# A two-layer decoder trunk on one core: matmul operands moved to multiples of 256 bytes, residual updates raised in VectorE's queue, 24 weight remainders formed by DMA, and matmuls of ones put first

## The chip, the core and the metric

The kernel runs on one core of a Trainium2 chip. The metric is the device time of one execution in microseconds (us); a run before and a run after are compared by their medians. The engines are TensorE (PE: matmuls; PEld: its weight loads), VectorE (DVE), ScalarE (ACT), GpSimd (POOL) and SyncE (SP, which issues most DMAs). Each engine works off its own queue in order.

## The reference

The program computes two layers (DEPTH = 2) over 512 tokens of width 1024 in float32. Each layer has three steps, each added to the residual `x`:

```python
x = x + 0.5 * swiglu(rmsnorm(x, ffn1_norm[l]), w_gate, w_up, w_down)   # FFN of width 2816
x = x + hybrid_mixer(rmsnorm(x, mix_norm[l]), ...)                     # sparse attention | mLSTM heads, then w_out
x = x + 0.5 * swiglu(rmsnorm(x, ffn2_norm[l]), w_gate, w_up, w_down)
# swiglu(x) = (silu(x @ w_gate) * (x @ w_up)) @ w_down
```

So there are four FFNs and two mixers. The mixer has a projection of 3020 columns, an indexer that keeps 128 keys for each query, softmax attention, an mLSTM and an output projection.

## The kernel before

**Number format.** Every large product runs as three matmuls in a faster float32 form (`mm3`): each operand is split into a rounded part `hi` and a remainder `lo`, and `hi*hi + hi*lo + lo*hi` is accumulated. Three matmuls of one such product are called a triple below. A weight tile (a unit, 128 x 1024) comes by an SP DMA into `raw` (six buffers); `unit()` lets ACT round it into `whi` (line 267) and makes the remainder `wlo = raw - whi`. Mostly DVE does that (line 272). For units that are marked (the third field of a job) ACT writes `-whi` into `wlo` (line 269) and a DMA issued by POOL adds the weights from memory on top (line 270). Before, only units of the mixers were marked. `whi` and `wlo` have three buffers each, and units are prepared two ahead of the one in use.

**FFN.** `ffn_plan` lays out the order: gate and up units of block 0 (`U 0`, four units), then two units of block 1, two down units of block 0 (`D 0`), two more units of block 1, then groups of two blocks in which each block is seven products (`quad`, a Strassen-like scheme on halves of 256 columns, line 495) with down units (line 547, through `mm3`) between them. One `U` unit is 8 triples of 512 columns. One down unit of block 0 has four products of two triples, and each product goes to one of three PSUM buffers `aux`, which DVE empties by adding it to the residual (line 550, called an x update here). In the same stretch DVE works off `combine()`: scaled inputs `ys` (line 383), sums of halves `yc` (line 391) and remainders `yl`, `s4a` and `qT` (line 401), all needed by the later quads. The code of `combine()` stands ahead of the x updates, and a scheduler orders each engine's queue by priority, which follows the order of the code except where `high_priority` raises it.

**Where operands lie.** Tiles of the pool `act` get their place in SBUF in the order in which their tags are first used. In the built program the tiles `kT`, `big` and `h` (tag `s4b`), and `whi` and `wlo`, begin at multiples of 256 bytes in each partition; `qT` begins 64 bytes past one; `yh0` to `yh7`, `yl0` to `yl7`, `zah`, `zal` and the four `s4a` begin 128 bytes past one.

**Start.** SP issues x, three weight units, x in the other layout and a dozen small constants before the fourth weight unit. The tile `ones` is set by POOL.

Of the kernel before, what the change touches and what calls it, by code (L numbers as in the profile page):

```python
# [7 lines left out]
F32 = mybir.dt.float32  # L8
F32R = mybir.dt.float32r
I32 = mybir.dt.int32  # L10
AF = mybir.ActivationFunctionType
ALU = mybir.AluOpType
# [3 lines left out]
P = 128  # L16
S = 512
# [3 lines left out]
NKT = D // P  # L21
# [3 lines left out]
AH, AD = 8, 64  # L25
# [7 lines left out]
UN = 1024  # L33
# [2 lines left out]
HEADS = (("o", 0), ("qk", 0), ("qk", 1), ("qk", 2), ("o", 1), ("qk", 3), ("o", 2), ("o", 3))  # L36
PLAIN = ((0, 0), (0, 1), (1, 0), (1, 1))
H = S // 2
RAWS = 6
PRODUCTS = (("a11", "b11", 0, True), ("s2", "t2", 1, True), ("a12", "b21", 0, False), ("s1", "t1", 2, True),  # L40
            ("s3", "t3", 1, False), ("a22", "t4", 3, True), ("s4", "b22", 2, False))
# [17 lines left out]
class Trunk:  # L59
# [49 lines left out]
    def setup(self):  # L109
        nc, cp, t = self.nc, self.cp, self.t  # L110
        self.x = []
        self.stream = []
        self.jobs = []
        self.last = []
        self.plan = self.ffn_plan()
        for l in range(DEPTH):
            self.ffn_units(l, "1")
            n0 = len(self.jobs)
            for u in range(4):
                self.add(t["w_a"][l, u], 2 * C_A)  # L120
            for nm in ("w_q", "w_v"):
                for u in range(4):
                    self.add(t[nm][l, u])
            for nm, h in HEADS:
                if nm == "o":
                    self.add(t["w_o"][l, h])
                else:
                    for i in range(2):
                        self.add(t["w_qk"][l, 2 * h + i])
            for u in range(8):  # L130
                self.add(t["w_out"][l, u])
            for i in POOLU:
                self.jobs[n0 + i] = self.jobs[n0 + i][:2] + (True,)
            self.ffn_units(l, "2")
        self.made = 0
        self.loaded = []
        self.taken = 0
        self.raws = []
        self.g1 = []
        for l in range(DEPTH):  # L140
            g = cp.tile([P, NKT], F32, name=f"g1_{l}", tag=f"g1_{l}")
            nc.scalar.dma_start(g, t["g1"][l])
            self.g1.append(g)
        warm = cp.tile([P, 1], F32, name="warm", tag="warm")
        nc.vector.memset(warm, 0.0)
        nc.scalar.activation(warm, warm, AF.Silu)
        with self.tc.high_priority(offset=20000):
            for i in range(NKT):
                xt = cp.tile([P, S], F32, name=f"x{i}", tag=f"x{i}")
                nc.sync.dma_start(xt, t["x"][i])  # L150
                self.x.append(xt)
                if i in START:
                    self.fetch()
            self.xt = []
            for b in range(NB):
                xt = self.ap_.tile([P, D], F32, name="xt", tag=("s4b", "s4b", "so", "so")[b], bufs=2)
                nc.sync.dma_start(xt, t["xt"][b])
                self.xt.append(xt)

        def const(nm, shape, src):  # L160
            c = cp.tile(shape, F32, name=nm, tag=nm)
            nc.sync.dma_start(c, src)
            return c

        self.zid = cp.tile([P, 3 * P], F32R, name="zid", tag="zid")
        z = self.tmp()[:, 0:3 * P]
        nc.sync.dma_start(z, t["ident"])
        nc.scalar.activation(self.zid, z, AF.Copy)
        z = self.zid.bitcast(F32)
        self.ident = z[:, P:2 * P]  # L170
        self.pick = cp.tile([32 + MH, MH], F32R, name="pick", tag="pick")
        nc.vector.tensor_tensor(out=self.pick, in0=z[0:32 + MH, P:P + MH], in1=z[0:32 + MH, P + 32:P + 32 + MH],
                                op=ALU.add)
        self.ones = cp.tile([P, P], F32, name="ones", tag="ones")
        nc.gpsimd.memset(self.ones, 1.0)
        self.abias = const("abias", [P, P], t["abias"])
        self.rope = const("rope", [P, NB, 2 * AD], t["rope"])
        self.gm = [const(f"gm_{l}", [P, NKT], t["gm"][l]) for l in range(DEPTH)]
        self.g2 = [const(f"g2_{l}", [P, NKT], t["g2"][l]) for l in range(DEPTH)]
        self.cw = [const(f"cw_{l}", [P, 8, 5], t["cw"][l]) for l in range(DEPTH)]  # L180
        self.mn = [const(f"mn_{l}", [P, MH], t["mn"][l]) for l in range(DEPTH)]
# [12 lines left out]
                plan += [("D", gi - 1, u) for n, u in at if n == 7]  # L194
        return plan + [("D", len(GROUPS) - 1, u) for u in range(4)]

    def add(self, src, n=UN):
        self.jobs.append((self.plain, (self.raw(src, n), n), False))

    def raw(self, src, n=UN):  # L200
        self.stream.append((src, n))
# [3 lines left out]
    def ffn_units(self, l, n):  # L205
        t = self.t
        for kind, b, i in self.plan:
            if kind == "U":
                m, u = PLAIN[i]
                self.add(t["w" + "gu"[m] + n][l, b, u])  # L210
            elif kind == "D":
                self.add(t["wda" + n][l, i] if b == 0 else t["wdb" + n][l, b - 1, i])
            else:
                if i == 0:
                    q = {}
# [322 lines left out]
    def ffn_down(self, h, nf, u):  # L538
        nc = self.nc
        w = UN // nf  # L540
        hi, lo = self.unit()
        for j in range(w // P):
            d = u * (w // P) + j
            ps = self.pa.tile([P, S], F32, name="aux", tag="aux")
            for f in range(nf):
                c = slice(f * w + j * P, f * w + (j + 1) * P)
                self.mm3(ps, (hi[:, c], lo[:, c]), (h[0][:, f, :], h[1][:, f, :]), f == 0, f == nf - 1)
                if f % 2:
                    self.tick()
            nc.vector.scalar_tensor_tensor(self.x[d], ps, 0.5, self.x[d], op0=ALU.mult, op1=ALU.add)  # L550


    def mixer(self, l):
# [594 lines left out]
```

## Time and profile before

| | |
|---|---|
| time, median of 3 runs (lowest to highest) | 1961.65 us (1958.77 to 1962.58) |
| time of the profiled execution | 1961.55 us |
| its span, first to last instruction | 1959.9 us |
| mean granted TensorE clock | 0.988 |
| PE busy | 1911.9 us, 98% of the span |
| VectorE busy | 1394.3 us, 71% |
| ScalarE busy | 943.7 us, 48% |
| GpSimd busy | 511.2 us, 26% |

Busy time of TensorE counts from a matmul's start to its modelled end, and consecutive matmuls overlap; so a busy share near 100% says that matmuls followed each other without a gap, not how quickly. How quickly is read from the distances between their starts. Waits of TensorE, with what ended them, are in the view of waits.

### The profile page before, as it was taken

The numbers are of one execution on the slowest core, as the hardware profiler recorded it, in microseconds if no ns is written. First come the engines' busy times: TensorE is split into PE (matmuls) and PEld (weight loads), VectorE is DVE, ScalarE is ACT, GpSimd is POOL, SyncE is SP. The second block draws the span as 40 slices with busy tenths as digits, with TensorE's granted clock in tenths as the row PEclk, the third lists the DMA queues.
The fourth block names the chain that finished last, engine by engine and source line by source line (L and its number), as shares of the span: only waits on it lengthen the run. The fifth ranks groups of instructions, "written<-read, shape, count | busy, mean of one in ns | idle before, by whom it ended". The sixth has DMA issues, their size and how long they took to land.

```text
span 1959.9 us, 29399 instructions
## 1 busy us (share of the span) xinstructions
PE 1911.9 (98%) x11672; PEld 1698.4 (87%) x11672; DVE 1394.3 (71%) x2242; ACT 943.7 (48%) x1481; POOL 511.2 (26%) x306
## 2 busy tenths in 40 slices
PE   8899999999999999999999999999999999999999
PEld 6799999887887799999878999998888877999997
DVE  7866667589955886666788666665898558866665
ACT  5344344577765444343444343446677644443432
POOL 0332322212113132333203423312211121433330
PEclk9899999999999999999999999999999999999999
DMA  7132323474346232322321323334643452332322
GB/s 256 58 109 95 120 76 126 117 152 108 87 108 140 76 108 76 119 100 94 119 86 61 123 81 114 109 112 125 146 108 87 109 128 65 108 108 87 121 74 86
DMA packets 60473, 209.82 MB, mean 107 GB/s; under 512 B 7984, under 2 KB 8496, under 8 KB 60336
## 3 DMA queue, kind: packets, MB, share of 16 engines
q1 hardware_dynamic: 51696, 178.44, 27.1%
q0 software_dynamic: 8064, 29.36, 9.2%
q8 instruction: 91, 1.49, 0.3%
q14 instruction: 46, 0.38, 0.1%
q10 hardware_dynamic: 576, 0.15, 0.1%
HBM read 205.83 MB, written 2.10 MB: 106 GB/s over the span
## 4 chain that ended last, share of the span: by engine, by line
PE 85%; DVE 10%; ACT 2%; issue 2%; POOL 0%; DMA 0%; DVEq 0%; SPq 0%; ACTq 0%; POOLq 0%
PE mm L495 36%; PE aux L289 26%; PE mm L289 22%; DVE sc L843 2%; PE op L289 1%; DVE m L842 1%; DVE wlo L272 1%; PE aux L892 1%; DVE yl L401 0%; DVE x L1075 0%; DVE yc L391 0%; DVE sc L832 0%; DVE x L550 0%; DVE big L332 0%; ACT tmp L329 0%
## 5 line engine op out<-in xcount | busy, mean ns | idle before, releaser
L267 ACT ACTIVATE whi<-raw 128x1024 fp32r<-128x1024 f32 (+1 forms) x292 | 308.3, 1056 | 478.7 <-PE aux L289 213.3
L272 DVE TENSOR_TENSOR wlo<-raw,whi 128x1024 fp32r<-128x1024 f32 (+1 forms) x236 | 309.8, 1313 | 102.0 <-ACT whi L267 98.2
L244 POOL TENSOR_TENSOR ws<-raw 128x1024 f32<-128x1024 f32 x72 | 194.5, 2702 | 641.5 <-DVE wlo L272 457.1
L495 PE MATMUL mm<-yh,wlo 128*128 128x256 f32 x1152 | 324.5, 282 | 0.0
L495 PE MATMUL mm<-yl,whi 128*128 128x256 f32 x1152 | 324.5, 282 | 0.0
L495 PE MATMUL mm<-yh,whi 128*128 128x256 f32 x1152 | 324.3, 282 | 0.0
L272 DVE TENSOR_TENSOR wlo<-ws,whi 128x1024 fp32r<-128x1024 f32 x144 | 219.0, 1521 | 98.3 <-ACT whi L267 98.1
L267 ACT ACTIVATE whi<-ws 128x1024 fp32r<-128x1024 f32 x144 | 152.8, 1061 | 264.2 <-PE mm L495 127.1
L550 DVE SCALAR_TENSOR_TENSOR x<-aux,x 128x512 f32<-128x512 f32 x192 | 129.9, 686 | 136.2 <-PE aux L289 135.9
L495 PEld LDWEIGHTS mm<-yh,whi 128*128 128x128 f32 x1152 | 216.9, 188 | 2.0 <-ACT pT L516 0.7
L495 PEld LDWEIGHTS mm<-yl,whi 128*128 128x128 f32 x1152 | 216.7, 188 | 1.4
L495 PEld LDWEIGHTS mm<-yh,wlo 128*128 128x128 f32 x1152 | 216.9, 188 | 0.0
L495 PE MATMUL mm<-qT,whi 128*128 128x256 f32 x1152 | 205.6, 280 | 0.7 <-DVE lg L527 0.7
L495 PEld LDWEIGHTS mm<-qT,whi 128*128 128x128 f32 x1152 | 177.8, 188 | 3.8 <-issue 1.4
L495 PE MATMUL mm<-qT,wlo 128*128 128x256 f32 x576 | 160.8, 279 | 0.0
L289 PE MATMUL aux<-zah,whi 128*128 128x512 f32 x384 | 151.6, 395 | 0.0
L289 PE MATMUL aux<-zal,whi 128*128 128x512 f32 x384 | 151.6, 395 | 0.0
L289 PE MATMUL aux<-zah,wlo 128*128 128x512 f32 x384 | 151.6, 395 | 0.0
L244 POOL TENSOR_TENSOR ws<-ws,raw 128x1024 f32<-128x1024 f32 x36 | 89.8, 2493 | 115.9 <-issue 115.6
L495 PEld LDWEIGHTS mm<-qT,wlo 128*128 128x128 f32 x576 | 108.1, 188 | 0.0
L289 PE MATMUL mm<-yh,whi 128*128 128x512 f32 x256 | 106.4, 416 | 0.0
L495 PE MATMUL mm<-s4a,whi 128*128 128x256 f32 x576 | 104.7, 282 | 0.0
(287 smaller groups left out, 4216.5 us busy)
## 6 DMA issues: line engine op xcount, KB each, us to landing
raw<-wg_dram SPq DMA_DIRECT2D x88, 512.0 KB, 3.6
raw<-wu_dram SPq DMA_DIRECT2D x88, 512.0 KB, 3.7
raw<-wdb_dram SPq DMA_DIRECT2D x80, 512.0 KB, 3.6
raw<-w_qk_dram SPq DMA_DIRECT2D x16, 512.0 KB, 3.2
wlo<-w_qk_dram POOLq DMA_DIRECT2D x16, 512.0 KB, 5.4
raw<-w_out_dram SPq DMA_DIRECT2D x16, 512.0 KB, 3.2
wlo<-w_out_dram POOLq DMA_DIRECT2D x16, 512.0 KB, 5.8
raw<-wda_dram SPq DMA_DIRECT2D x8, 512.0 KB, 3.6
```

Of the source, the lines that this page charges most:

```text
L244: self.tc.keep_in_program_order(self.nc.gpsimd.tensor_tensor(out=out, in0=x, in1=y, op=op))
L267: nc.scalar.activation(hi[:, :n], raw, AF.Copy)
L272: nc.vector.tensor_tensor(out=lo[:, :n], in0=raw, in1=hi[:, :n].bitcast(F32), op=ALU.subtract)
L289: self.nc.tensor.matmul(ps, lhsT, rhs, start=start, stop=stop)
L495: nc.tensor.matmul(ps[:, f, :], a[:, c], r, start=first and f == 0 and k == 0 and n == 0, stop=k == 3 and n == 2, skip_group_check=True)
L550: nc.vector.scalar_tensor_tensor(self.x[d], ps, 0.5, self.x[d], op0=ALU.mult, op1=ALU.add)
L842: nc.vector.max(out=m8, in_=sc)
L843: nc.vector.match_replace(out=sc, in_to_replace=m8, in_values=sc, imm_value=MARK)
L892: nc.tensor.transpose(pt[:, j * P:(j + 1) * P], it["lg"][:, j * P:(j + 1) * P], self.ident)
```

## The change

Four edits.

1. In `setup`, the tags of the operand tiles of the pool `act` (`yh`, `yl`, `zah`, `zal`, `kT`, `qT`, `s4a`, `s4b`) are used first, in an order in which all of them begin at multiples of 256 bytes (read from the built program; `big` too). Nothing is computed by it.
2. The x update of a down unit is issued with a raised priority.
3. Six units of each FFN, the four of block 1 and the two of `D 0`, get their remainder from ACT and an accumulating POOL DMA in place of DVE.
4. `ones` is set ahead of the loads, and 16 matmuls of `ones` by `ones` (128 x 128) stand first in TensorE's queue. Their result is not used.

```diff
+WARM = 16
@@ setup
+        for tag, shape, n in ([(f"y{c}{i}", [P, S], 1) for i in range(NKT) for c in "hl"] +
+                              [("zah", [P, 4, S], 1), ("zal", [P, 4, S], 1), ("kT", [P, 4, S], 1),
+                               ("qT", [P, AH, S], 1), ("s4a", [P, S], 4), ("s4b", [P, UN], 2)]):
+            for _ in range(n):
+                self.ap_.tile(shape, F32R, name=tag, tag=tag, bufs=n)
         warm = cp.tile([P, 1], F32, name="warm", tag="warm")
         nc.vector.memset(warm, 0.0)
         nc.scalar.activation(warm, warm, AF.Silu)
+        self.ones = cp.tile([P, P], F32, name="ones", tag="ones")
+        nc.gpsimd.memset(self.ones, 1.0)
+        with self.tc.manual_schedule(engines={mybir.EngineType.PE}):
+            ps = self.pa.tile([P, S], F32, name="aux", tag="aux")
+            for _ in range(WARM):
+                self.mm(ps[:, 0:P], self.ones, self.ones, True, True)
...
-        self.ones = cp.tile([P, P], F32, name="ones", tag="ones")
-        nc.gpsimd.memset(self.ones, 1.0)
@@ add, ffn_units
-    def add(self, src, n=UN):
-        self.jobs.append((self.plain, (self.raw(src, n), n), False))
+    def add(self, src, n=UN, dma=False):
+        self.jobs.append((self.plain, (self.raw(src, n), n), dma))
...
-                self.add(t["w" + "gu"[m] + n][l, b, u])
+                self.add(t["w" + "gu"[m] + n][l, b, u], dma=b == 1)
             elif kind == "D":
-                self.add(t["wda" + n][l, i] if b == 0 else t["wdb" + n][l, b - 1, i])
+                self.add(t["wda" + n][l, i] if b == 0 else t["wdb" + n][l, b - 1, i], dma=b == 0)
@@ ffn_down
-            nc.vector.scalar_tensor_tensor(self.x[d], ps, 0.5, self.x[d], op0=ALU.mult, op1=ALU.add)
+            with self.tc.high_priority(offset=500):
+                nc.vector.scalar_tensor_tensor(self.x[d], ps, 0.5, self.x[d], op0=ALU.mult, op1=ALU.add)
```

Each engine's order changes only in the first part of each FFN (and at the program's start). VectorE in the first FFN, around the first x updates, before (`x_83` is the first of the eight tiles of x, `yl` and `s4a` are remainders of combine):

```order
L391 TENSOR_TENSOR yc<-ys,yc 128x512 x2
L401 TENSOR_TENSOR yl_353<-ys,yh_352 128x512
L401 TENSOR_TENSOR yl_345<-yc,yh_344 128x512
L401 TENSOR_TENSOR yl_347<-yc,yh_346 128x512
L401 TENSOR_TENSOR yl_355<-ys,yh_354 128x512
L391 TENSOR_TENSOR ys<-ys 128x2x256 x2
L391 TENSOR_TENSOR yc<-yc,ys 128x512 x2
L401 TENSOR_TENSOR yl_365<-yc,yh_364 128x512
L401 TENSOR_TENSOR yl_367<-yc,yh_366 128x512
L550 SCALAR_TENSOR_TENSOR x_83<-aux,x_83 128x512
L550 SCALAR_TENSOR_TENSOR x_87<-aux,x_87 128x512
```

The same place now (`x_131` is the first tile of x; L561 is the x update, L411 and L401 are combine, L485 a step of the gate of block 1):

```order
L401 TENSOR_TENSOR yc<-ys,yc 128x512 x2
L481 TENSOR_TENSOR lg<-mm,rsb 128x512 x2
L411 TENSOR_TENSOR yl_393<-yc,yh_392 128x512
L561 SCALAR_TENSOR_TENSOR x_131<-aux,x_131 128x512
L485 TENSOR_TENSOR lg<-lg,rsb 128x512
L411 TENSOR_TENSOR yl_395<-yc,yh_394 128x512
L561 SCALAR_TENSOR_TENSOR x_135<-aux,x_135 128x512
L485 TENSOR_TENSOR lg<-lg,rsb 128x512
L561 SCALAR_TENSOR_TENSOR x_137<-aux,x_137 128x512
L411 TENSOR_TENSOR yl_401<-ys,yh_400 128x512
L561 SCALAR_TENSOR_TENSOR x_139<-aux,x_139 128x512
L411 TENSOR_TENSOR yl_403<-ys,yh_402 128x512
```

The first x update stood behind all sums and eight remainders of combine; it now stands behind four sums and three remainders, and the rest alternates with the following x updates. In the other three FFNs it stands behind all of combine (one pair, `s4a`, more than before), but without the five weight remainders (line 272) that lay between.

ScalarE in the first FFN, where the first marked units are prepared, before (`rsb` is the row of inverse norms that the gate waits for):

```order
L168 ACTIVATE zid<-tmp 128x384
L267 ACTIVATE whi<-raw 128x1024 x3
L365 ACTIVATE rsb<-aux 128x512
L474 ACTIVATE lg<-lg 128x512 x2
L267 ACTIVATE whi<-raw 128x1024
```

And now:

```order
L180 ACTIVATE zid<-tmp 128x384
L277 ACTIVATE whi<-raw 128x1024 x2
L279 ACTIVATE wlo<-whi 128x1024
L277 ACTIVATE whi<-raw 128x1024
L279 ACTIVATE wlo<-whi 128x1024
L375 ACTIVATE rsb<-aux 128x512
```

Two more activations (L279, the negated `whi` of the units `U 1 0` and `U 1 1`) stand ahead of `rsb`. On POOL the six accumulating DMAs stand ahead of the first sum of weights (line 244) of their FFN; SP's order is unchanged.

## Rows read from the trace of the kernel before

**Rows 1.** The chain of work that ended last, by line, from the page.

```profile
PE mm L495 36%; PE aux L289 26%; PE mm L289 22%; DVE sc L843 2%; PE op L289 1%; DVE m L842 1%; DVE wlo L272 1%; PE aux L892 1%; DVE yl L401 0%; DVE x L1075 0%; DVE yc L391 0%; DVE sc L832 0%; DVE x L550 0%; DVE big L332 0%; ACT tmp L329 0%
```

**Rows 2.** Waits of PE: for whom, us in total, times, longest.

```profile
PE aux L289 <- DVE x L550: 14.0, 4, 8.0
...
PE aux L289 <- POOL tmp L330: 6.1, 3, 2.7
```

**Rows 3.** Timeline of PE at three borders: start us, us, engine, operation.

```profile
948.69 0.39 PE L289 MATMUL aux<-kT,whi 128*128 128x512 f32 x1
...
959.60 0.40 PE L289 MATMUL aux<-zah,whi 128*128 128x512 f32 x1
...
981.99 0.39 PE L289 MATMUL mm<-kT,whi 128*128 128x512 f32 x1
```

**Rows 4.** Timeline of PE at three borders between products of quads.

```profile
928.66 0.28 PE L495 MATMUL mm<-yh,whi 128*128 128x256 f32 x1
...
940.05 0.40 PE L495 MATMUL mm<-s4a,whi 128*128 128x256 f32 x2
...
943.03 0.40 PE L495 MATMUL mm<-qT,whi 128*128 128x256 f32 x2
```

**Rows 5.** Groups of PE by form: count, busy us, mean ns of one, idle before.

```profile
L495 PE MATMUL mm<-yh,whi 128*128 128x256 f32 x1152 | 324.3, 282 | 0.0
L495 PE MATMUL mm<-qT,whi 128*128 128x256 f32 x1152 | 205.6, 280 | 0.7 <-DVE lg L527 0.7
...
L289 PE MATMUL aux<-zah,whi 128*128 128x512 f32 x384 | 151.6, 395 | 0.0
...
L289 PE MATMUL aux<-kT,wlo 128*128 128x512 f32 x256 | 100.0, 390 | 0.0
```

**Rows 6.** Timeline of PE at the fourth product of `D 0`, first and third FFN.

```profile
47.91 0.39 PE L289 MATMUL aux<-h,wlo 128*128 128x512 f32 x1
56.32 1.22 PE L289 MATMUL aux<-h,whi 128*128 128x512 f32 x2 [8.02 <-DVE x L550]
...
1026.70 0.39 PE L289 MATMUL aux<-h,wlo 128*128 128x512 f32 x1
1029.08 0.72 PE L289 MATMUL aux<-h,whi 128*128 128x512 f32 x2 [2.00 <-DVE x L550]
```

**Rows 7.** Stretches: length, busy (count) of PE, PEld, DVE, ACT, POOL; PEclk, DMA, GB/s.

```profile
50.70:61.00 10.30, 4.68 (x11) 3.72 (x12) 9.66 (x16) 2.29 (x3) 1.56 (x3) 0.50 0.00 0
...
1030.40:1033.80 3.40, 3.40 (x10) 2.66 (x9) 3.11 (x5) 1.06 (x1) 0.00 (x0) 0.50 0.00 0
```

**Rows 8.** The same view: the stretches ahead of the first x update, FFN one and two.

```profile
29.70:55.60 25.90, 18.60 (x82) 14.91 (x80) 25.84 (x41) 12.39 (x19) 0.00 (x0) 0.91 0.38 133
643.30:671.40 28.10, 26.86 (x118) 21.69 (x116) 27.96 (x41) 15.35 (x23) 0.00 (x0) 1.00 0.30 93
```

**Rows 9.** A remainder on DVE (timeline), and a rounding on ACT (costliest groups).

```profile
34.14 1.23 DVE L272 TENSOR_TENSOR wlo<-raw,whi 128x1024 fp32r<-128x1024 f32 x1
...
L267 ACT ACTIVATE whi<-raw 128x1024 fp32r<-128x1024 f32 (+1 forms) x292 | 308.3, 1056 | 478.7 <-PE aux L289 213.3
```

**Rows 10.** Line 270: an issue's ns min/median/max, and all issues' landing.

```profile
L270 POOL DMA_DIRECT2D wlo<-w_qk_dram x16: 849/876/895, 443.8 to 1500.3; - x16
...
DMA to landing us min/median/max: 5.2/5.5/7.5
```

**Rows 11.** Timeline of SP, PE and ACT at the start of the program.

```profile
20.99 0.43 SPq L227 DMA_DIRECT2D raw<-wu_dram  x1
...
25.74 0.73 PE L289 MATMUL mm<-qT,whi 128*128 128x512 f32 x2 [0.93 <-ACT whi L267]
...
26.11 1.06 ACT L267 ACTIVATE whi<-raw 128x1024 fp32r<-128x1024 f32 x1 [0.42 <-DMA raw<-wg_dram]
...
33.03 0.39 PE L289 MATMUL mm<-kT,whi 128*128 128x512 f32 x1
```

**Rows 12.** A stretch as in group 7, while the first FFN's weights load.

```profile
28.00:32.00 4.00, 4.00 (x17) 2.93 (x17) 3.92 (x6) 2.31 (x4) 0.00 (x0) 1.00 1.03 410
```

## The prediction

> **What bounds the kernel now.** I read the chain first, then who waited for whom, then the distances between TensorE's starts. Of the chain that ended last the three largest shares are TensorE's, 84% together; VectorE's key selection in the mixers (lines 842 and 843) has 3% [rows 1]. Its waits are short: the largest is for DVE's x update, 14.0 us in four waits; another 6.1 us goes to POOL's sum of squares at the norms, which no edit touches [rows 2]. So nearly all of the time is the rate of the matmuls, and that differs between operands of one shape. From 948.69 two down units (48 matmuls of 512 columns) read `kT` and `big`, which begin at multiples of 256 bytes; 10.91 us later, at 959.60, four units (96) begin that read `zah` and `zal`, 128 bytes off, and last until 981.99, 22.39 us [rows 3]. That is 227.3 ns a matmul against 233.2. The mean durations differ alike, 390 against 395 ns [rows 5]. Of 256 columns, four products (96 matmuls) on `yh` and `yl`, 128 bytes off, take 11.39 us, 118.6 ns each [rows 4]; two on `qT`, 64 bytes off, run from 943.03 to 948.69, 117.9 ns each [rows 3, 4]. No aligned operand of 256 columns is in the trace.
>
> **Edit 1, addresses.** At 512 columns the matmuls with an operand 128 bytes off are: 1152 of down units, 768 on `yh`/`yl` in the mixers, 192 on `zah`/`zal` in the output projection, and 384 token projections in which the stationary operand is off; together 2496, by the counts of triples in the code. I take 5.4 ns each (between 5 by durations and 5.9 by starts): 13.5 us. Another 384 on `qT`, 64 bytes off, I give a third of that, 0.7 us. At 256 columns there are 1152 x 3 on `yh`/`yl` and 288 x 3 on `s4a`, 4320 in all, and 1728 on `qT` (of the first group a third stands in [rows 5], of `qT` two thirds). The price is unknown there. From below it is nothing. From above it is the whole 5.9 ns a matmul: aligned ones would take 118.6 - 5.9 = 112.7, and `qT`, at 117.9, would gain 5.2; 25.5 + 9.0 = 34.5 us. I take half of the 512-column price for half of the columns, 2.6 ns, and 1.5 for `qT`: 11.2 + 2.6 = 13.8 us. While VectorE's key selection is the chain [rows 1] a faster TensorE only waits longer; I allow 1.5 us for it, half of what the 576 channel-projection matmuls of 512 columns would give. Sum of edit 1: 13.5 + 0.7 + 13.8 - 1.5 = 26.5 us, from 12.7 to 47.2.
>
> **Edits 2 and 3, the start of each FFN.** `D 0` writes eight products into three buffers, so the fourth needs the first x update. In the first FFN it begins at 56.32 where the one before began at 47.91: without the wait it would have been 0.23 us later, so 8.2 us are lost, and the clock then stays at 0.50 of full speed until 61, which takes half of 4.7 us, 2.3. In the others 2.15 us are lost each (1029.08 - 1026.70 - 0.23), in the third and fourth also half of a 3.4 us stretch at 0.50, 1.7 each [rows 2, 6, 7]. What is late is DVE: ahead of that update it is busy 25.84 of 25.90 us in the first FFN and 27.96 of 28.10 in the second [rows 8].
>
> The change takes weight remainders out of that stretch, 1.23 us each [rows 9]. In the second FFN five go, 6.1 us, and the pair `s4a` (1.3) comes ahead, so the update can run 4.8 us earlier, and it was 2.15 us late; the wait is gone. In the first FFN the update also passes ten operations of combine. Counted from `rsb`, which on ACT now follows four activations of 1.06 us that begin at 26.11 [rows 9, 11] and so comes near 30.9, 25 operations of 0.63 us (25.84 us over 41) lie ahead of it: 46.7, plus about a microsecond for ACT's roundings, 47.7. The fourth product could begin at 48.1, so this wait goes too, narrowly. What combine still owes is not late: after the eighth update six operations are left, about 5 us, and the quads begin two units, 10.9 us, later. Each x update now holds up what stands behind it on DVE until its product ends, at most 1.36 us; behind it are those same remainders.
>
> In place of DVE's 1.23 us a marked unit needs ACT twice (1.06 us) and a POOL issue (0.88 us) from whose start the landing takes 5.5 us, 7.5 at most [rows 9, 10]: 7.6 to 9.6 us. A buffer of `whi` comes free two units, 10.9 us, ahead of its use, and ACT has 1 to 2 us of other work in between. So it lies beside TensorE in FFNs two to four, with one or two us to spare. A rule of the Trainium skill speaks against it (SBUF — State Buffer, "SBUF: two separate sides"): a DMA issued by GpSimd needs descriptors that it cannot write while VectorE holds the port that they share. The landing times of the mixers hold whatever VectorE did there, so the longest, 7.5 us, stands in for it [rows 10].
>
> In the first FFN the same path is tight. Its first marked unit is rounded from 26.11 and negated by 28.2; 5.5 to 7.5 us on, it lands at 33.7 to 35.7, while the unit begins at 33.03 and reads `wlo` in its third matmul, at 33.5 [rows 11]. Besides, the DMA engines are full (share 1.03) until 32 [rows 12]. I take 2 us of new wait, from 0.2 to 4. Sum of edits 2 and 3: 8.2 + 2.3 - 2 + 3 x 2.15 + 2 x 1.7 = 18.3 us, from 16.3 to 20.1. The 24 remainders taken off DVE (29.5 us) and given to ACT (25 us) count for nothing more, since neither bounds the rest of an FFN.
>
> **Edit 4, matmuls of ones.** They may lift the clock before the real matmuls begin. But TensorE then waits at 25.74 for a weight unit that SP only issues at 20.99, behind the constants [rows 11], and SP's order stays: whatever is gained before is waited away. I take 0, at most 1 either way.
>
> **Sum.** 26.5 + 18.3 = 44.8 us. The profiled execution took 1961.55 us, 1.65 more than its span and 0.1 less than the median. 1961.6 - 44.8 = 1917.
>
> **Rivals.**
> A, the addresses do nothing: the 5.4 ns come from something else that goes with those tiles, such as what the other engines do at the time. For it: no aligned 256-column row exists, and no row tells of an address. Against it: `kT` and `zah` alternate in the same stretch [rows 3], and `qT`, 64 bytes off, is a little faster than `yh` at the same width [rows 3, 4]. Then 18.3 us remain: 1943. On a page this is the rule: the Trainium skill (TensorE: Matmul & The Clock Gate, "Back-to-back issue gap") gives an isolated gap of N/2.4 + 2.5 ns, 215.8 ns for 512 columns, with no term for an address; the trace has 227.3 and 233.2 [rows 3], so both carry more than it allows. Chance 0.11.
> B, the accumulating DMAs become the bound, slower than before. With three buffers, every third unit waits for what its path takes beyond 10.9 us; six units make two such waits in an FFN. All four FFNs must lose 44.8 us, 11.2 each, 5.6 a wait: a path of 16.5 us, which is a landing of 13 us with 3.5 for ACT and POOL. From there on it is slower; at 15 us it would be 2 x 4 x 2 = 16 us slower, 1978. The longest landing of 56 was 7.5 [rows 10]. Chance 0.04.
> C, the wait for the x update is only replaced by one for remainders at every FFN's start, and edit 1 works: 1961.6 - 26.5 = 1935. The narrow first FFN speaks for it, the spare time of the others against. Chance 0.05.
> D, A and C together: no change. Chance 0.03.
>
> **How the numbers follow.** Main case 0.77, by itself 1898 to 1932: 47.2 + 20.1 = 67.3 us at the one end (1894, with little chance), 12.7 + 16.3 = 29 at the other. The range 1900 to 1938 adds C and leaves out A, B and D (0.18). A difference under 0.2% (3.9 us) can't be told from none. Faster: main, A and C, 0.93; same: D, 0.03; slower: B, 0.04.
>
> **What would show it.** Edit 1: starts of `zah` and `kT` equally far apart (near 227 ns) and 256-column products near 116 ns; the surest sign against it is `zah` still at 233. Edits 2 and 3: no wait of PE for the x update in the view of waits, and no stretch at clock 0.50 near `D 0`. The new path: a wait of PE for the DMA's `wlo` near 33 us in the first FFN, and none in the other three. Edit 4: the first real matmuls at full clock, and the matmul at 25.74 where it was. The prediction is wrong if the rate at 256 columns moves by far more or less than 2.6 ns, or if landings in the FFNs take over 8 us.

## The result, and the profile after

The changed kernel takes 1942.41 us (median of 3 runs, 1942.06 to 1942.75), the kernel before 1960.53 us (median of 4): a ratio of 0.9909, 95% interval 0.9895 to 0.9922. A fourth run of the changed kernel took 2639.08 us at a mean granted clock of 0.654, where the other three had 0.994, and is not counted. The change saves 18.1 us, less than half of the 44.8 us forecast, and the time lies outside the range of 1900 to 1938. It is within 1 us of what rival A named (1943); whether for its reason is settled below. The profiled execution took 1942.07 us, its span is 1940.3 us.

The chain that ended last, by line, from the page of the changed kernel. It is what [rows 1] was: TensorE's matmuls have 81% in the three largest shares.

```profile
PE mm L505 35%; PE aux L299 26%; PE mm L299 20%; DVE sc L854 2%; DVE m L853 1%; PE op L299 1%; DVE wlo L282 1%; PE aux L903 1%; ACT whi L277 1%; POOL ws L254 1%; DMA wlo<-wg_dram 0%; DVE x L1086 0%; DVE sc L843 0%; DMA row<-nrow_dram 0%; DVE lg L918 0%
```

The starts of PE at the same six borders as [rows 3, 4], changed kernel.

```profile
919.97 0.28 PE L505 MATMUL mm<-yh,whi 128*128 128x256 f32 x1
...
931.49 0.40 PE L505 MATMUL mm<-s4a,whi 128*128 128x256 f32 x2
...
934.42 0.40 PE L505 MATMUL mm<-qT,whi 128*128 128x256 f32 x2
...
940.18 0.40 PE L299 MATMUL aux<-kT,whi 128*128 128x512 f32 x1
...
951.09 0.39 PE L299 MATMUL aux<-zah,whi 128*128 128x512 f32 x1
...
972.85 0.39 PE L299 MATMUL mm<-kT,whi 128*128 128x512 f32 x1
```

Divide the distances as before. The 96 matmuls on `zah` and `zal` take 21.76 us, 226.7 ns each (233.2 before); the 48 on `kT` and `big`, whose place did not change, take 10.91 us, 227.3 ns, as before. That is the gain the change was to bring. But of 256 columns the 96 on `yh` and `yl` take 11.52 us, 120.0 ns each (118.6 before), and the 48 on `qT` 5.76 us, 120.0 ns (117.9 before). At this width aligned operands are **slower**. The mean durations say the same, though faintly [rows 5]:

```profile
L505 PE MATMUL mm<-yh,whi 128*128 128x256 f32 x1152 | 326.2, 283 | 0.0
L505 PE MATMUL mm<-qT,whi 128*128 128x256 f32 x1152 | 209.1, 283 | 0.5
L299 PE MATMUL aux<-zah,whi 128*128 128x512 f32 x384 | 149.8, 390 | 0.0
```

Waits of PE in the whole program (us, times, longest): the two largest of the changed kernel, and the one on the new path. No wait for the x update is left [rows 2].

```profile
PE aux L299 <- POOL tmp L340: 7.4, 3, 3.1
PE op L299 <- ACT pT L905: 6.6, 7, 1.5
...
PE mm L299 <- DMA wlo<-wg_dram: 2.6, 1, 2.6
```

At the fourth product of `D 0` in the first FFN, where TensorE stood for 8 us [rows 6], one matmul now follows the other:

```profile
54.50 0.39 PE L299 MATMUL aux<-h,wlo 128*128 128x512 f32 x1
54.73 0.62 PE L299 MATMUL aux<-h,whi 128*128 128x512 f32 x2
```

The start of the program, timeline of SP, PE and POOL, to be read against [rows 11].

```profile
21.62 0.43 SPq L237 DMA_DIRECT2D raw<-wu_dram  x1
...
26.44 0.73 PE L299 MATMUL mm<-qT,whi 128*128 128x512 f32 x2 [1.65 <-ACT whi L277]
...
29.19 1.03 POOL L280 DMA_DIRECT2D wlo<-wg_dram  x1 [6.49 <-ACT wlo L279]
31.21 0.86 POOL L280 DMA_DIRECT2D wlo<-wg_dram  x1 [0.99 <-ACT wlo L279]
...
38.52 0.79 PE L299 MATMUL mm<-kT,wlo 128*128 128x512 f32 x1 [2.59 <-DMA wlo<-wg_dram]
```

The last row is the wait that is new: the first marked unit's remainder comes 9.3 us after its issue at 29.19. The landing of all accumulating DMAs of line 280, to be read against [rows 10], and of the two on `wg` in the first 70 us (count, size, median us to landing):

```profile
DMA to landing us min/median/max: 5.1/5.5/10.5
```

```profile
wlo<-wg_dram POOLq DMA_DIRECT2D x2, 512.0 KB, 9.9
```

Stretches of the first FFN, columns as in [rows 7]: two new stretches at clock 0.50 (1.2 of 2.4 GHz), each at or behind the end of a wait of TensorE (1.65 us at 26.44, 2.59 us at 38.52), none any more near `D 0`, and a stretch as in [rows 12].

```profile
28.21:31.62 3.41, 3.41 (x7) 2.01 (x7) 0.00 (x0) 3.17 (x4) 1.44 (x2) 0.50 1.02 418
38.45:41.86 3.41, 3.33 (x8) 2.66 (x9) 3.41 (x6) 1.04 (x2) 0.52 (x1) 0.50 1.05 285
50.70:61.00 10.30, 10.30 (x47) 8.55 (x46) 10.09 (x18) 5.73 (x7) 1.71 (x2) 1.00 0.88 196
...
28.00:32.00 4.00, 4.00 (x10) 2.46 (x9) 0.26 (x1) 3.47 (x4) 1.82 (x2) 0.57 1.03 422
```

Where the time went, from the first start of a 256-column matmul in an FFN to the last (us):

| stretch | before | after | difference |
|---|---|---|---|
| up to the first quad | 76.4 | 72.4 | -4.0 |
| quads and down units, each of four FFNs | 258.5 | 259.3 | +0.8 (four times) |
| mixer 1 and the start of FFN 2 | 355.2 | 349.0 | -6.2 |
| the start of FFN 3 | 100.0 | 95.6 | -4.4 |
| mixer 2 and the start of FFN 4 | 356.7 | 348.9 | -7.8 |
| the end | 37.6 | 37.1 | -0.5 |

Added up, with the second row four times, they are -19.7 us, the difference of the spans (-19.6). Half of the time of the program is in the quads, and there the change loses.

### The profile page after: what moved, and what is told of

Read it like the earlier page. It is cut to its first block, busy times and chain, and to the rows that moved or that the text cites. A ratio compares the mean times of both kernels' runs of the same rounds, so it can differ in the third digit from the quotient of the medians.

```text
span 1940.3 us, 29523 instructions
## 1 busy us (share of the span) xinstructions
PE 1904.4 (98%) x11704; PEld 1704.7 (88%) x11704; DVE 1373.5 (71%) x2218; ACT 964.7 (50%) x1505; POOL 533.1 (27%) x330
## 4 chain that ended last, share of the span: by engine, by line
PE 84%; DVE 9%; issue 3%; ACT 2%; POOL 1%; DMA 1%; ACTq 0%; DVEq 0%; POOLq 0%
PE mm L505 35%; PE aux L299 26%; PE mm L299 20%; DVE sc L854 2%; DVE m L853 1%; PE op L299 1%; DVE wlo L282 1%; PE aux L903 1%; ACT whi L277 1%; POOL ws L254 1%; DMA wlo<-wg_dram 0%; DVE x L1086 0%; DVE sc L843 0%; DMA row<-nrow_dram 0%; DVE lg L918 0%
## 5 line engine op out<-in xcount | busy, mean ns | idle before, releaser
L282 DVE TENSOR_TENSOR wlo<-raw,whi 128x1024 fp32r<-128x1024 f32 (+1 forms) x212 | 281.8, 1329 | 101.6 <-ACT whi L277 97.5
L561 DVE SCALAR_TENSOR_TENSOR x<-aux,x 128x512 f32<-128x512 f32 x192 | 130.8, 688 | 133.2 <-PE aux L299 132.7
L505 PEld LDWEIGHTS mm<-yh,whi 128*128 128x128 f32 x1152 | 221.0, 192 | 1.6
L505 PEld LDWEIGHTS mm<-yl,whi 128*128 128x128 f32 x1152 | 221.0, 192 | 1.2
L505 PEld LDWEIGHTS mm<-yh,wlo 128*128 128x128 f32 x1152 | 221.0, 192 | 0.0
```

The lines of the kernel that those rows point to most:

```text
L282: nc.vector.tensor_tensor(out=lo[:, :n], in0=raw, in1=hi[:, :n].bitcast(F32), op=ALU.subtract)
L505: nc.tensor.matmul(ps[:, f, :], a[:, c], r, start=first and f == 0 and k == 0 and n == 0, stop=k == 3 and n == 2, skip_group_check=True)
```

## The experiments

All are made from the changed kernel. A rate is given for a triple, three successive matmuls, as the distance of their starts: before, 680 ns on `kT` and 700 on `zah` at 512 columns. An offset is that of a tile's first byte past a multiple of 256 bytes. A time without an interval beside it is that of one run; the six runs of e2 spread over 6.5 us, and the kernel before, measured anew beside the experiments, had medians from 1958.94 to 1962.08 us, so differences of a few us between two experiments are not told from noise, while the distances of the starts are.

**e2: without edit 1.** The block of tags is taken out.

```diff
-        for tag, shape, n in ([(f"y{c}{i}", [P, S], 1) for i in range(NKT) for c in "hl"] + ...):
-            for _ in range(n):
-                self.ap_.tile(shape, F32R, name=tag, tag=tag, bufs=n)
```

> The changed kernel without its first edit, so with the addresses of the kernel before; the other three edits stay. Theory 1: 512 columns go back to some 233 ns (12.7 us lost), 256 columns back to 118.6 (yh) and 117.9 (qT) from 120.0 (8.3 us won back): 1946.8 us, so edit 1 as a whole is worth 4.4 us. Theory 2 (256 columns were slowed by another edit): they stay at 120.0 ns, and the time is 1955 us.

1944.43 us, ratio to before 0.9922 (0.9907 to 0.9937). The starts of PE at the borders:

```profile
921.76 0.28 PE L500 MATMUL mm<-yh,whi 128*128 128x256 f32 x1
...
933.15 0.40 PE L500 MATMUL mm<-s4a,whi 128*128 128x256 f32 x2
...
952.70 0.40 PE L294 MATMUL aux<-zah,whi 128*128 128x512 f32 x1
...
975.09 0.39 PE L294 MATMUL mm<-kT,whi 128*128 128x512 f32 x1
```

96 matmuls in 11.39 us, 118.6 ns, and 96 in 22.39 us, 233.2 ns: both are those of before to the last digit, with edits 2 to 4 in place. So it is edit 1 that changes the rates, at both widths, in opposite directions. As a whole it is worth about 2 us (1944.43 - 1942.41, not measured side by side; the runs of this one spread from 1940.7 to 1947.2), less than the 4.4 us that theory 1 asked for. Edits 2 to 4 bring 15.1 us by this run (1959.56 - 1944.43).

**e3: the operands of the quads 64 bytes off.** The big tiles first, so that `yh`, `yl`, `qT` and `s4a` begin behind `big`, whose size leaves 64 bytes.

```diff
-        for tag, shape, n in ([(f"y{c}{i}", [P, S], 1) for i in range(NKT) for c in "hl"] +
-                              [("zah", ...), ("zal", ...), ("kT", ...), ("qT", ...), ("s4a", ...), ("s4b", ...)]):
+        for tag, shape, n in ([("zah", ...), ("zal", ...), ("kT", ...), ("s4b", ...), ("big", ...)] +
+                              [(f"y{c}{i}", [P, S], 1) for i in range(NKT) for c in "hl"] +
+                              [("qT", ...), ("s4a", ...)]):
```

> The operands of the quads (yh, yl, qT, s4a) 64 bytes past a multiple of 256, all other operands on multiples. Theory 1: 256 columns at 117.7 ns in place of 120.0, 6048 matmuls, 14 us won; the 512-column matmuls that read yh, yl and qT in the mixers lose 2.3 ns each, 3 to 4 us in all: about 1932 us. Theory 2: 256 columns stay at 120.0 ns, 1945 us.

1932.97 us, ratio 0.9861 (0.9842 to 0.988). The starts:

```profile
917.84 0.28 PE L506 MATMUL mm<-yh,whi 128*128 128x256 f32 x1
...
929.15 0.40 PE L506 MATMUL mm<-s4a,whi 128*128 128x256 f32 x2
```

11.31 us for 96, 117.8 ns. Theory 1's time and rate, and 9.4 us below the changed kernel.

**e1: a ladder of offsets.** `yh`/`yl` two by two at 0, 32, 64 and 128 bytes, `s4a` and `zah` at 192, `kT` and `big` at 128, `qT` at 64 (tags in this order, with small tiles between to shift them; `four(i)` stands for `yh` and `yl` of i and i + 1, `small` is a tile of 64 bytes in each partition, `pad0` and `pad1` have 32):

```diff
+        for tag, shape, n in (four(0) + [("pad0", [P, 8], 1)] + four(2) + [("pad1", [P, 8], 1)] + four(4) +
+                              [("widx", small, 1)] + four(6) + [("g_b", small, 1)] +
+                              [("s4a", [P, S], 4), ("zah", ...), ("zal", ...), ("g_u", small, 1), ("g_em", small, 1),
+                               ("qT", ...), ("g_mpb", small, 1), ("kT", ...), ("s4b", ...), ("big", ...)]):
```

> Operands at several offsets within 256 bytes in one program: yh/yl 0 and 1 at 0, 2 and 3 at 32, 4 and 5 at 64, 6 and 7 at 128, s4a and zah/zal at 192, qT at 64, kT and big at 128. Theory 1 (the offset of the moving operand sets the rate, with the order of the offsets turned round between the widths): products of 256 columns take 120.0 ns a matmul at offset 0, about 117.7 at 64, 117 to 120 at 128, and differ within one quad; at 512 columns zah and kT go to 229 ns or more. Theory 2 (the rate at 256 columns comes from another edit or from the load on the other engines): all products of a quad take one and the same rate, 120.0 ns. Time: by theory 1 some 1940 to 1950 us, since the 512 columns get slower again and the 256 columns partly faster; by theory 2 about 1955.

1944.04 us. Within one quad the four products on `yh` have the rates 360 (0 bytes), 353 (32), 353 (64) and 351 to 361 (128); `s4a`, at 192, has 340, a rate not seen before; `zah`, at 192, has 700. So the rate does go by the offset. But `qT`, always at 64, has 353 behind down units on `kT` and 340 behind those on `zah`: the offset does not fix it alone. Two products on `qT` (48 matmuls), behind `zah` and behind `kT`, each with the start of what follows:

```profile
118.77 0.39 PE L511 MATMUL mm<-qT,whi 128*128 128x256 f32 x2
...
124.21 0.28 PE L511 MATMUL mm<-yh,whi 128*128 128x256 f32 x1
...
180.39 0.28 PE L511 MATMUL mm<-qT,whi 128*128 128x256 f32 x1
...
186.04 0.28 PE L511 MATMUL mm<-yh,whi 128*128 128x256 f32 x1
```

5.44 us (340 a triple) and 5.65 us (353).

**e4: only the weights moved.** `whi`, `wlo` and `raw` 64 bytes off, the rest aligned.

```diff
+        self.wp.tile([P, 16], F32, name="pad", tag="pad", bufs=1)
-        for tag, shape, n in ([(f"y{c}{i}", [P, S], 1) for i in range(NKT) for c in "hl"] +
+        for tag, shape, n in ([("gp", [P, 32], 1), ("widx", [P, 16], 1)] +
+                              [(f"y{c}{i}", [P, S], 1) for i in range(NKT) for c in "hl"] +
```

> Only the weights whi, wlo and raw are moved, to 64 bytes past a multiple of 256; yh, yl, qT, zah, kT and the rest stay on multiples. Theory 1 in its narrow form (only the operand that is streamed counts): nothing changes for channel projections, 226.7 and 120.0 ns, about 1942 us; only the 384 token projections, where the weights are streamed, get slower, 1 to 2 us. Theory 3 (either operand counts alike): 256 columns go to about 118 ns and 512 columns to 229 ns or more, about 1940 us with both rates shifted.

1930.98 us. The starts:

```profile
914.72 0.28 PE L507 MATMUL mm<-yh,whi 128*128 128x256 f32 x1
...
925.60 0.39 PE L507 MATMUL mm<-s4a,whi 128*128 128x256 f32 x2
...
945.59 0.39 PE L301 MATMUL aux<-zah,whi 128*128 128x512 f32 x1
...
967.99 0.39 PE L301 MATMUL mm<-kT,whi 128*128 128x512 f32 x1
```

10.88 us for 96, 113.3 ns (340 a triple), and 22.40 us for 96, 233.3 ns. Theory 1 falls in its narrow form: the streamed operands lie where they lay, and the rates of both widths have changed. Theory 3 is right that either operand counts, but not in its rates: it asked for about 118 ns at 256 columns, and for 1940 us. The rates are those of a streamed operand at 192 with the weights at 0 (the ladder's `s4a` and `zah`), which led to theory 4: the difference of the offsets counts.

**e10: everything 64 bytes off.** As e4, and the other operands moved by 64 bytes too.

```diff
-        for tag, shape, n in ([("gp", [P, 32], 1), ("widx", [P, 16], 1)] +
+        for tag, shape, n in ([("gp", [P, 32], 1), ("widx", [P, 16], 1), ("g_b", [P, 16], 1)] +
```

> Weights and all other operands 64 bytes past a multiple of 256, so that the difference of the two is that of the changed kernel. Theory 7: only the difference counts; triples of 680 ns at 512 columns and 360 ns at 256, and 1942 us. Rival: the offset of either operand by itself counts; weights 64 off made 700 and 340 with the others at 0, others 64 off made 687 and 353 with the weights at 0, and the two together would make something else, by the sum of the two 707 and 333.

1943.77 us. The starts:

```profile
921.89 0.28 PE L507 MATMUL mm<-yh,whi 128*128 128x256 f32 x1
...
933.41 0.40 PE L507 MATMUL mm<-s4a,whi 128*128 128x256 f32 x2
...
953.01 0.39 PE L301 MATMUL aux<-zah,whi 128*128 128x512 f32 x1
...
974.77 0.39 PE L301 MATMUL mm<-kT,whi 128*128 128x512 f32 x1
```

11.52 us (120.0 ns) and 21.76 us (226.7 ns), the changed kernel to the digit. The rival's sum, 707 and 333 ns a triple, did not come. Being a multiple of 256 bytes is worth nothing by itself; equal offsets of weights and streamed operand make 226.7 and 120.0, at 64 bytes as at 0.

**e5: the operands of the quads at 192, the rest aligned.** As e3, with the tile `gp` (128 bytes) ahead of `yh`.

```diff
-                               ("s4b", ...), ("big", ...)] +
+                               ("s4b", ...), ("big", ...), ("gp", [P, 32], 1)] +
```

> The operands of the quads (yh, yl, qT, s4a) 192 bytes past a multiple of 256, the weights and all other operands on multiples. Theory 4, formed after the run with moved weights: the difference of the two operands' offsets sets the rate, and a streamed operand 192 bytes ahead of the weights is the quickest at 256 columns (three matmuls in 340 ns) and the slowest at 512 (700 ns). Then the 2016 triples of 256 columns win 19 to 20 ns each against the changed kernel, 38 to 40 us; in the mixers 384 triples of 512 columns on yh and qT lose 20 ns, 7.7 us, and 156 token projections lose 7 ns, 1.1 us: 1942.4 - 30 = 1912 us. Theory 1 (only the streamed operand's own offset counts, 64 bytes off is the best that was seen with the weights in place): s4a at 192 in the ladder ran at 340 for another reason, and the time is no better than that of quads 64 bytes off, 1933 us.

1934.31 us, ratio 0.9858 (0.9842 to 0.9875): 22 us worse than theory 4 asked for, and close to theory 1's 1933. The starts:

```profile
915.64 0.28 PE L506 MATMUL mm<-yh,whi 128*128 128x256 f32 x1
...
926.94 0.40 PE L506 MATMUL mm<-s4a,whi 128*128 128x256 f32 x2
...
929.90 0.39 PE L506 MATMUL mm<-qT,whi 128*128 128x256 f32 x2
...
935.34 0.39 PE L300 MATMUL aux<-kT,whi 128*128 128x512 f32 x1
...
946.24 0.39 PE L300 MATMUL aux<-zah,whi 128*128 128x512 f32 x1
...
968.00 0.39 PE L300 MATMUL mm<-kT,whi 128*128 128x512 f32 x1
```

In one quad, at one difference, `yh` runs at 117.7 ns (11.30 us for 96; 353 a triple) and `qT` at 113.3 (5.44 us for 48; 340). Between them the first triple on `s4a` took 570 ns, a short stop; behind it the rate is 340 until the next down units. So at a difference of 192 there are two rates, as the ladder's `qT` had at 64, and theory 4 in its simple form, one price for each difference, falls.

**e6: a second ladder.** `yh`/`yl` at 96, 160, 224 and 32, `zah` and `big` at 32, `kT` at 224, `qT` and the second pair at 160, `s4a` at 96.

```diff
+        for tag, shape, n in ([("pad0", [P, 8], 1), ("zah", ...), ("zal", ...), ("widx", small, 1)] +
+                              four(0) + [("s4a", [P, S], 4), ("g_b", small, 1)] + four(2) +
+                              [("qT", ...), ("g_u", small, 1)] + four(4) +
+                              [("kT", ...), ("g_em", small, 1)] + four(6) + [("s4b", ...), ("big", ...)]):
```

> A second ladder, for the offsets that were not seen: yh/yl 0 and 1 and s4a at 96, yh/yl 2 and 3 and qT at 160, yh/yl 4 and 5 and kT at 224, yh/yl 6 and 7 and zah/zal and big at 32, weights at 0. Theory 4 asks for one price by offset: at 256 columns between 353 and 360 ns a triple at 32 and 96, near 340 to 355 at 160 and 224; at 512 columns 680 to 690 at 32 and 690 to 703 at 160 and 224. Rival: the price follows the product that ran before (as qT at 64 bytes off took 340 behind zah and 353 behind kT in the first ladder), and no offset has a price of its own. Time 1935 to 1955 us, of no weight.

1954.91 us. At 512 columns all of them take about 700 ns a triple, `zah` at 32 bytes too, for which theory 4 asked 680 to 690. At 256 columns triples lie between 350 and 364. None of these offsets is better than those already known; the rival, that the price depends on what ran before, is not told apart here.

**e13 and e14: what fixes the rate at 192.** Quads at 192, the operands of the down units at 64 (e13) and at 128 (e14), and the two units of e7 on VectorE.

```diff
-        for tag, shape, n in ([(f"y{c}{i}", [P, S], 1) for i in range(NKT) for c in "hl"] + ...
+        for tag, shape, n in ([("widx", [P, 16], 1), ("zah", ...), ("zal", ...), ("kT", ...), ("s4b", ...), ("big", ...),
+                               ("g_b", [P, 16], 1)] +
+                              [(f"y{c}{i}", [P, S], 1) for i in range(NKT) for c in "hl"] + ...
```

(e14 has `gp` in the place of `widx` and no `g_b`.)

> Weights at 0, the operands of the quads 192 bytes off, those of the down units (zah, zal, kT, big, h) 64 bytes off, and the first FFN's first two marked units on VectorE. Theory 9: at a difference of 192 a quad runs at 340 or 353 ns a triple, and it is the aligned down units (difference 0) that bring it to 353; behind units with another difference it stays at 340. Then against the version with all differences at 192 (1925.4 us) some 896 down triples win 13 ns each: 1914 us. Rival: any change of the difference between down units and quads brings 353: 1925.4 - 11.6 + 2016 x 12.5 ns = 1939 us.

> The same with the operands of the down units 128 bytes off. Theory 9: quads at 340 ns, down units at 696 in place of 700, 1922 us. Rival: quads at 353, 1947 us.

e13 1934.05 us, ratio 0.9873 (0.9857 to 0.989), e14 1923.48 us. The first two starts are e13's, from `yh` to `s4a`, the others e14's, each from its own timeline.

```profile
913.88 0.28 PE L506 MATMUL mm<-yh,whi 128*128 128x256 f32 x1
...
925.18 0.40 PE L506 MATMUL mm<-s4a,whi 128*128 128x256 f32 x2
```

```profile
911.68 0.28 PE L506 MATMUL mm<-yh,whi 128*128 128x256 f32 x1
...
922.56 0.39 PE L506 MATMUL mm<-s4a,whi 128*128 128x256 f32 x2
```

11.30 us (353 a triple) behind down units at 64, 10.88 us (340) behind those at 128. Theory 9 and its rival both fall: aligned down units are not alone in bringing the slower rate, and not any change brings it. What the five runs with quads at a difference of 192 (e4, e5, e9, e13, e14) have in common: behind down units that run at 680 or 687 a triple the quads run at 353, save behind a stop as in e5, and behind those at 692 to 704 they run at 340. Whether it is the rate of the down units or their difference that counts is not told apart, and the ladder's `qT` at 64 does not follow this: it has 353 behind `kT`, whose triples there take 697 to 700.

**e7: the first two marked units of the first FFN on VectorE.**

```diff
-                self.add(t["w" + "gu"[m] + n][l, b, u], dma=b == 1)
+                self.add(t["w" + "gu"[m] + n][l, b, u], dma=b == 1 and (l, n, i) not in ((0, "1", 0), (0, "1", 1)))
```

> The changed kernel with the first FFN's first two marked units (the only ones prepared while the first weights load) back on VectorE. Theory 5: TensorE's wait of 2.59 us at 38.52 for the accumulating DMA and the stretch at half clock behind it (half of 3.4 us) go, and the first quad begins some 4 us earlier, at 68.4 in place of 72.4. Rival: the two remainders, 2.5 us, are on VectorE again ahead of the first x update, and TensorE waits there instead: the first quad begins at 70.5 to 72.4. The time is that much below 1942.4 us.

1935.37 us. The first quad:

```profile
68.11 0.28 PE L505 MATMUL mm<-yh,whi 128*128 128x256 f32 x1
```

It begins 4.3 us ahead of the changed kernel's (72.41), as theory 5 asked: 2.59 us of wait and half of the 3.41 us at clock 0.50. No wait for the x update came in its place. The single run is 7.0 us below 1942.4; another 1.7 us of it are a stretch at half clock in mixer 1 of the changed kernel (628.96 to 632.37) that this trace does not have, which may be chance.

**e8: without the matmuls of ones.**

```diff
-        with self.tc.manual_schedule(engines={mybir.EngineType.PE}):
-            ps = self.pa.tile([P, S], F32, name="aux", tag="aux")
-            for _ in range(WARM):
-                self.mm(ps[:, 0:P], self.ones, self.ones, True, True)
```

> The changed kernel without the 16 matmuls of ones. Theory 6 (they cost nothing and bring nothing, since TensorE waits for a weight unit at 26 us in either case): the unit on qT begins within 0.3 us of where it was before the change, and the time is that of the changed kernel within 1 us. Rival (they cost): the stretch at half clock from 28.21 to 31.62 goes, 1.7 us, and the late start of 0.7 us with it, 2.4 us faster.

1943.03 us. Timeline of PE:

```profile
26.03 0.73 PE L295 MATMUL mm<-qT,whi 128*128 128x512 f32 x2 [0.36 <-ACT whi L273]
...
38.20 0.50 PE L295 MATMUL mm<-kT,wlo 128*128 128x512 f32 x1 [4.28 <-DMA wlo<-wg_dram]
```

The unit on `qT` begins 0.29 us behind that of before (25.74), as theory 6 had it. The stretch at half clock at 28 us is gone, as the rival had it, and the start is 0.4 us earlier than the changed kernel's; but the wait for the accumulating DMA is 4.28 us in place of 2.59, and the first quad begins at 72.1 (72.4). Whatever comes earlier is waited away at 38 us: nothing won, nothing lost. Whether the matmuls of ones cost anything once that wait is gone (e7 has a stretch at half clock from 27.6 to 31.0 us) was not tried.

**e11: without edit 3, and e12: without edit 2.**

```diff
-                self.add(t["w" + "gu"[m] + n][l, b, u], dma=b == 1)
+                self.add(t["w" + "gu"[m] + n][l, b, u])
```

```diff
-            with self.tc.high_priority(offset=500):
-                nc.vector.scalar_tensor_tensor(self.x[d], ps, 0.5, self.x[d], op0=ALU.mult, op1=ALU.add)
+            nc.vector.scalar_tensor_tensor(self.x[d], ps, 0.5, self.x[d], op0=ALU.mult, op1=ALU.add)
```

(e11 also leaves out the mark on the units of `D 0`.)

> The changed kernel without its third edit: all weight remainders of the FFNs on VectorE, the x update still raised. Theory 8 (in FFNs two to four it was the five remainders that made the x update late, and the raised priority alone passes none of them): TensorE waits for the x update 2 to 3.5 us in each of these three, and in the first FFN up to 3 us; the wait for the accumulating DMA in the first FFN goes. Some 1946 to 1952 us. Rival (the raised priority does it): no wait for the x update, 1938 us.

> The changed kernel without its second edit: the six units by DMA stay, the x update has its old priority. Theory 8: in FFNs two to four no wait for the x update (6.1 us of remainders are gone, it was 2.15 us late); in the first FFN, where the x update stands behind ten operations of combine (6.3 us) again, a wait of 2 to 6 us; 1944 to 1949 us. Rival (the priority does it): the waits of 2 us in FFNs two to four return, over 1949 us.

e11 1942.67 us, e12 1947.53 us. The first row is e11's, the second e12's:

```profile
75.90 0.39 PE L505 MATMUL mm<-yh,whi 128*128 128x256 f32 x1 [1.99 <-ACT pT L526]
```

```profile
57.89 1.22 PE L299 MATMUL aux<-h,whi 128*128 128x512 f32 x2 [4.53 <-DVE x L560]
```

In FFNs two to four neither run has a wait for the x update: theory 8 is right on e12 and wrong on e11. Either edit alone removes these waits. In the first FFN it is edit 2 that is needed (e12 waits 4.53 us there). Without edit 3 the first quad begins at 68.0 in place of 72.4; what that wins is lost again by the wait of 1.99 us and 3.4 us at half clock inside that FFN's quads, which take 263.0 us in place of 259.3. So, by these single runs, edit 3 as it was made brings no time that edit 2 does not bring. Without its first two units it does: e7, too, begins its first quad at 68.1, and its quads in that FFN take 259.3 us, 3.7 less than e11's.

**e9: the best of both**, e4 and e7 together.

> The moved weights (64 bytes past a multiple of 256, everything else on multiples) together with the first FFN's first two marked units back on VectorE. Theory: the two are independent, since one sets the rate of the matmuls and the other takes one wait away. Moved weights alone stood at 1931.0, the first FFN alone won 4.3 us ahead of its first quad: 1925 to 1927 us. Rival: the quicker quads only wait elsewhere, 1930 us.

1925.44 us (1923.65 to 1926.67), ratio to before 0.9818 (0.9805 to 0.9831): 17 us below the changed kernel, in the range that the theory named and 5.5 us below e4's single run. Its quads take 253.4 us an FFN (259.3), as e4's do. But that the two gains add up is shown for the time alone: the first quad begins at 69.98 us, 1.7 us ahead of e4's (71.67) and not 4.3. The wait for the accumulating DMA (2.63 us in e4, with no stretch at half clock behind it) is gone, but the unit on `qT` began 1.0 us later than in e4 (27.40 against 26.40). The rest of the 5.5 us lies behind the first FFN's quads.

## Why the prediction was wrong

**The step that failed is the price of edit 1 at 256 columns**: "I take half of the 512-column price for half of the columns", with nothing as its lower end. It should have had the other sign. By the rows, 4320 matmuls lost 1.4 ns and 1728 on `qT` 2.1 ns: 6.0 + 3.6 = 9.6 us (about 8 by the means over all triples) where 13.8 us of gain were forecast. That is 22 to 23 of the missing 25.4 us, and since the range's far end for edit 1 was 12.7 us of gain, it could not hold the result. Of this width there were two rows, 118.6 ns at 128 bytes and 117.9 at 64 [rows 3, 4]; I continued them to an offset of 0, where no row stood, because 512 columns were fastest there.

**At 512 columns the step was right in sign, and somewhat large**: 6.5 ns a matmul on `zah` in the rows shown, 5.4 as the mean over all of them, but only some 2.6 on `yh` and `yl` in the mixers; 11 to 13 us over all, against 13.5 + 0.7. Rival A (addresses do nothing) is refuted by e2 and e4, and that its 1943 us came all the same is chance: the gain at 512 columns and the loss at 256 largely cancel. What counts is not the address against 256 bytes but its difference from that of the weights (e10).

**Edits 2 and 3 in FFNs two to four were right in size**: the three waits and the two stretches at half clock are gone, 9.85 us by the prediction's own terms. The reason given, five remainders less on VectorE, was only one of two sufficient ones (e11). Either edit alone removes these waits, so the two are not two gains. Rival C, a wait that takes the place of the other, did not come in these FFNs.

**In the first FFN a term was mis-sized**: 8.5 us were forecast (8.2 + 2.3 - 2), 4.0 came. The old wait went with its clock, 10.3 us. But the new wait was 2.59 us, with 1.7 us of clock behind it that the term left out, the start was 0.7 us later (26.44 against 25.74) and another stretch at half clock cost 1.7: 6.7 us, not 2. The two accumulating DMAs landed after 9.3 and 10.5 us, not 7.5, past the 8 us that the prediction had named as a sign against it; the medians of these two lie between 9.7 and 10.5 us in every run that kept them. In FFNs two to four the landings took 5.8 to 7.4 us (medians by group, singly 5.4 to 7.7), about what the prediction had taken. When the long ones were issued the DMA engines were full (share 1.03, 422 GB/s). That this is the cause is not shown: from 1013.90 to 1017.30 us the share is 1.00 too, at 235 GB/s, and the accumulating DMA issued at 1011.3 landed after 5.7 us. The port rule of the Trainium skill that it weighed (SBUF — State Buffer, "SBUF: two separate sides") does not account for the long ones: while POOL issued them, from 28 to 32 us, VectorE did one operation of 0.26 us.

**Edit 4 was right**: nothing, because the next wait takes it (e8). But the matmul that was to stay at 25.74 began at 26.44, and 0.4 of these 0.7 us are gone without the matmuls of ones (e8).

By the measured terms: 11 to 13, less 8, plus 9.85 and 4.0, make 17 to 19 us, in which what edit 1 gained in the first FFN counts twice; the medians say 18.1. Measured as a whole, edit 1 brings 2 us and edits 2 to 4 bring 15.1 (e2). Whether the rest of the 4.4 us that e2's theory 1 worked out from the rates did not arrive, or is lost in the spread of e2's runs, is open. Rivals B and D did not come. The allowance of 1.5 us for the key selection was not tried by itself.

## What to carry to other kernels

A lower bound of zero needs a row, as much as any other number does, and a time that fits a rival is no proof of its reason. Where a form does not occur in the trace (aligned operands of 256 columns here), the sign is open, and a small run with that form costs less than an argument. Read the rate of a full TensorE from distances between starts, for each shape and operand apart; try placements of weights against streamed operands as one parameter, and judge by the sum over all shapes. A DMA that is hidden in the steady state must be priced again at the start of the program, while the first weights load, with the clock that a stop costs behind it.

## What the runs showed of the hardware

- The rate of a chain of weight load and matmul depends on the difference of the two operands' offsets within 256 bytes, as far as pairs with one difference were tried: 0 (both at 0, both at 64 in e10) and 192 (weights at 0 in e1, at 64 in e4). Triples at the full clock, by their most frequent values, streamed operand less weights: 0: 680 ns at 512 columns and 360 at 256; 64: 687, and 353 or 340 (e1); 128: 690 to 706 and 351 to 361; 192: about 700, and 340 or 353. Of 0, 64 and 192 the one that is better at one width is worse at the other; 128 is the best at neither. Why was not found; so was not why 64 and 192 have two rates at 256 columns, except that they go with the units that ran before (e1, e5, e13, e14) and that the rate changes at a short stop (e5).
- The Trainium skill (TensorE: Matmul & The Clock Gate, "Back-to-back issue gap") gives N/2.4 + 2.5 ns for an isolated gap; worked out for 512 and 256 columns that is an estimate of 215.8 and 109.2 ns. No run here reached it: the least means over a product or a down unit were 226.7 and 113.3 ns.
- An accumulating DMA of 512 KB landed after 5.5 us at the median of 80 and after up to 10.5 us while the first weights loaded.
